# Attention by pairs of heads: fp32 probabilities and values in two halves of TensorE's columns, row sums in four strips

## The chip, the cores and the metric

One core of a Trainium2 chip runs the whole program. The metric is the device time of one execution in microseconds (us). Five engines matter here: TensorE (PE, matmuls; PEld is its loading of weights), VectorE (DVE), ScalarE (ACT), GpSimd (POOL) and SyncE (SP, which starts most DMAs).

## What is computed

The program is a two-block network on 512 tokens of width 1024. The change touches one part of the second block: grouped-query attention of 768 tokens (256 of a context, 512 latent) with 16 query heads of 64 features and 4 key and value heads. Latent queries see all 768 keys, context queries only the 256 of the context.

```python
Q_WIDTH = ATTN_HEADS * HEAD_DIM          # 16 heads of 64
def gqa_attend(q, k, v):
    s = jnp.einsum('bkgqd,bksd->bkgqs', q, k, preferred_element_type=jnp.float32) * (HEAD_DIM ** -0.5)
    p = jax.nn.softmax(s, axis=-1).astype(v.dtype)
    return jnp.einsum('bkgqs,bksd->bkgqd', p, v)
```

All numbers are fp32.

## The kernel before

An ordinary fp32 product is made of three products of a one-pass type, fp32r: a tensor x is split into a high part h (x rounded to fp32r) and a low part l = x - h, and `h·l + l·h + h·h` is summed in PSUM. In the rows such a product stands as three matmuls (L240: `hh,wl`, `hl,wh`, `hh,wh`). A few small matmuls keep plain fp32 operands; each of those leaves two records in the trace, for instance L1489, whose 96 matmuls in the program are 192 records.

`attn_proj` makes Q, K and V, `keys` transposes K into the parts `K2`, and `attend` is the attention. `V` is kept as `Vh` (128 keys x 65: 64 features and a column of ones) and `Vl` (64 features). `attend` is a generator with an order written out by hand at its end:

- `ahead(g)` prepares the pair of heads g = 0 to 7: it transposes the queries, makes their parts `q2` and `q1`, and finds the row maxima `mx` by whole score products (L1738, L1744, with a maximum on DVE each), which go into row 64 of `q1` by DMA so that the score product already has the maximum taken off.
- `scores(h, u)` is one head h and one step u. For u = 0 to 5, step u takes 128 keys against 512 latent queries; step 6 takes the two context key tiles against 256 context queries. Two matmuls (L1765, L1766) fill `st` (two PSUM buffers), ACT takes the exponential into `pr`, and `pr` is split into `ph` and `pl` on ACT, DVE or POOL by a fixed pattern.
- `values(h, u)` adds three matmuls into `acc`: `Vh·pl`, `Vl·ph`, `Vh·ph` (L1787 to L1789). The column of ones makes row 64 of `acc` the softmax's denominator. At u = 5 and u = 6 ACT copies rows 0 to 63 to `O` and row 64 to `sums`.
- `divide(g)` brings the sums to 12 x 128 by DMA, takes the reciprocal, spreads it by matmuls with `pick` (L1815) and multiplies (L1818).

The loop makes scores for (h, u) and values for the step three before; between them it advances `ahead` of the next pair by one yield, and every seventh step it advances `more`, the adaLN products (`mods`): plain fp32 matmuls of 128 x 32 weights (L1489), each in one of four strips of 32 columns of TensorE, `tile_position=(0, c)`, c = 0, 32, 64, 96.

A scheduler decides the final order on each engine from this program, so what stands side by side in the code need not stand side by side on an engine.

Of the kernel before, what the change touches and what calls it, by code (L numbers as in the profile page):

```python
# [9 lines left out]
F32 = mybir.dt.float32  # L10
F32R = mybir.dt.float32r
U32 = mybir.dt.uint32
AF = mybir.ActivationFunctionType
ALU = mybir.AluOpType
# [3 lines left out]
P = 128  # L18
D = 1024
L = 512  # L20
EPS = 1e-6
MIX = 512
C64 = 64
# [1612 lines left out]

def attn_proj(b, st, hs, t0, tabs, p2, w, Q, K, V):


    nc = b.nc  # L1640
    order = [4, 5, 0, 1, 2, 3]

    def take(i, t, acc):
        tab = tabs[t]
        t += t0
        i = order[i]
        a = acc.rearrange("p (h d) -> p h d", d=C64)
        if i == 5:
            h, l = (z[:, t, :, :C64] for z in V)
            nc.scalar.copy(h, a)  # L1650
            nc.vector.tensor_tensor(l, a, h.bitcast(F32), op=ALU.subtract)
            return
        sq = p2.tile([P, 4, C64], F32, tag="sq", name="sq")
        nc.scalar.activation(sq, a, AF.Square)
        s = p2.tile([P, 4], F32, tag="s", name="s")
        nc.vector.tensor_reduce(s, sq, axis=AX.X, op=ALU.add)
        o = (Q[i] if i < 4 else K)[:, t]
        n = 0 if i < 4 else 1
        if tab is None:
            nc.vector.tensor_tensor(o, a, w[:, 2 * n].unsqueeze(1).to_broadcast([P, 4, C64]), op=ALU.mult)  # L1660
        else:
            cos, sin = (z.unsqueeze(1).to_broadcast([P, 4, C64]) for z in tab[2 * n : 2 * n + 2])
            nc.vector.tensor_tensor(o, a, cos, op=ALU.mult)
            r = p2.tile([P, 4, C64], F32, tag="r", name="r")
            half = lambda z, f: z.rearrange("p h (x f i) -> p h x f i", x=2, f=2)[:, :, :, f]
            for f in range(2):
                nc.vector.tensor_tensor(half(r, f), half(a, 1 - f), half(sin, f), op=ALU.mult)
            nc.gpsimd.tensor_tensor(o, o, r, op=ALU.add)
        z = 1.0 / C64 if n else 1.0
        nc.vector.tensor_scalar(s, s, z, z * C64 * EPS, op0=ALU.mult, op1=ALU.add)  # L1670
        b.power(s, 4)
        nc.gpsimd.tensor_tensor(o, o, s.unsqueeze(2).to_broadcast([P, 4, C64]), op=ALU.mult)

    return st.tokens(b.a["w_qkv"], 8, hs, range(len(tabs)), order, take)


# [16 lines left out]
def attend(b, Q, K2, V, out, high, low, p2, psc, ctx, more):  # L1693

    nc = b.nc
    Vh, Vl = V
    T, n0 = 6 * P, 2 * P  # L1700
    old, new = slice(0, n0), slice(n0, T)
    ready = {}
# [51 lines left out]
            nc.sync.dma_start(q1[a][64:65].bitcast(F32).rearrange("o (t q) -> o t q", q=P), mr[6 * a : 6 * a + 6].bitcast(F32))  # L1754
        yield

    def scores(h, u):

        q2, q1 = (q[h % 2] for q in ready[h // 2][:2])
        K1 = ready[h // 2][2]  # L1760
        kv = h // 4
        p = pss.tile([P, 512], F32, tag="st", name="st")
        for k, q, o in [(u, new, p)] if u < 6 else [(k, old, p[:, k * n0 : (k + 1) * n0]) for k in range(2)]:
            c = slice(k * P, (k + 1) * P)
            nc.tensor.matmul(o, K1[:, c], q1[:, q], start=True, stop=False)  # L1765
            nc.tensor.matmul(o, K2[:, kv, c], q2[:, q], start=False, stop=True)  # L1766
        pr = p4.tile([P, 512], F32, tag="pr", name="pr")
        nc.scalar.activation(pr, p, AF.Exp)
        ph, pl = (pp.tile([P, 512], F32R, tag=z, name=z) for z in ("ph", "pl"))
        n = 7 * h + u  # L1770
        if n % 5 == 3:
            nc.scalar.copy(ph, pr)
        else:
            (nc.vector if n % 5 == 1 else nc.gpsimd).tensor_scalar(ph, pr, 1.0, 0.0, op0=ALU.mult, op1=ALU.add)
        (nc.vector if n % 3 == 1 else nc.gpsimd).tensor_tensor(pl, pr, ph.bitcast(F32), op=ALU.subtract)
        return ph, pl

    accs, sums, O, L = {}, {}, {}, {}

    def values(h, u, ph, pl):  # L1780
        kv = h // 4
        if u in (0, 6):
            accs[h] = psa.tile([P, 512], F32, tag="acc", name="acc")[:65, : 4 * P if u == 0 else n0]
        acc = accs[h]
        for k, x in [(u, slice(0, 512))] if u < 6 else [(k, slice(k * n0, (k + 1) * n0)) for k in range(2)]:
            first, last = k == 0, k == (1 if u == 6 else 5)
            nc.tensor.matmul(acc, Vh[:, k, kv], pl[:, x], start=first, stop=False)  # L1787
            nc.tensor.matmul(acc[:64], Vl[:, k, kv], ph[:, x], start=False, stop=False)
            nc.tensor.matmul(acc, Vh[:, k, kv], ph[:, x], start=False, stop=last)  # L1789
        if u < 5:  # L1790
            return
        g, r = h // 2, h % 2 * 64
        if u == 5 and h % 2 == 0:
            sums[g] = p1.tile([65, T], F32, tag="s", name="sums")
            O[g] = po.tile([P, T], F32, tag="O", name="O")
        at = new if u == 5 else old
        nc.scalar.copy(O[g][r : r + 64, at], acc[:64])
        nc.scalar.copy(sums[g][r : r + 1, at], acc[64:])
        if u == 6 and h % 2:
            parts.append(divide(h // 2))  # L1800
            next(parts[-1])

    def divide(g):
        inv = p2.tile([12, P], F32, tag="s", name="s")
        for a in range(2):
            nc.sync.dma_start(inv[6 * a : 6 * a + 6], sums[g][64 * a : 64 * a + 1].rearrange("o (t q) -> o t q", q=P))
        nc.vector.reciprocal(inv, inv)
        if g % 2 == 0:
            L[g // 2] = low.tile([P, 2, T], F32R, tag="l", name="ol")
        out.append((high.tile([P, T], F32R, tag="h", name="oh"), L[g // 2][:, g % 2]))  # L1810
        yield
        for c0, c1 in ((2, 6), (0, 2)):
            r = psc.tile([P, 512], F32, tag="ps", name="rt")[:, : (c1 - c0) * P]
            for t in range(c0, c1):
                nc.tensor.matmul(r[:, (t - c0) * P : (t - c0 + 1) * P], pick[:, t], inv, start=True, stop=True)  # L1815
            s = slice(c0 * P, c1 * P)
            o = O[g][:, s]
            nc.vector.tensor_tensor(o, o, r, op=ALU.mult)  # L1818
            b.parts(*(z[:, s] for z in out[g]), o)
        yield  # L1820
# [1 line left out]
    yield from ahead(0)  # L1822
    yield
    pq = b.pool("atq", 2, ctx=ctx)
    pp = b.pool("atp", 5, ctx=ctx)
    p4 = b.pool("at4", 4, ctx=ctx)
    pss, psa = (b.pool(f"ps2{n}", k, PSUM, ctx=ctx) for n, k in (("s", 2), ("v", 2)))
    po = b.pool("ato", 2, ctx=ctx)
    p1 = b.pool("at1", 1, ctx=ctx)
    pick = p1.tile([12, 6, P], F32, name="pick")  # L1830
    for t in range(6):
        nc.scalar.copy(pick[:, t].rearrange("p (a i) -> p a i", a=2),
                       b.ident[:12, t : t + 7 : 6].unsqueeze(2).to_broadcast([12, 2, 64]))
    todo = [(h, u) for h in range(16) for u in range(7)]
    made, parts, lead, side = [], [], 3, iter(())
    for i in range(len(todo) + lead):
        if i < len(todo):
            h, u = todo[i]
            made.append(scores(h, u))
            if h % 2 == 0 and u == 0 and h < 14:  # L1840
                side = ahead(h // 2 + 1)
        next(side, None)
        if i % 7 == 3:
            next(more, None)
        if i >= lead:
            values(*todo[i - lead], *made[i - lead])
            made[i - lead] = None
            if i == len(todo) + lead - 1 or i % 14 == 12 and i > 14:
                next(parts.pop())
    run(more)  # L1850

# [238 lines left out]
def block2(b, st, X, h, late, old_, c, out, ctx):  # L2090


    nc = b.nc
    n = 256
    T = n + L
    old, new = slice(0, n), slice(n, T)
# [7 lines left out]
    with ExitStack() as c0:  # L2104
# [3 lines left out]
        with ExitStack() as c1:  # L2108
            kp = b.pool("kv", 1, ctx=c1, side="right")
            K2 = kp.tile([P, 4, T], F32R, name="K2")  # L2110
            V = kp.tile([P, 6, 4, C64 + 1], F32R, name="Vh"), kp.tile([P, 6, 4, C64], F32R, name="Vl")
            nc.gpsimd.memset(V[0][:, :, :, C64:].bitcast(F32), 1.0)
            K = kp.tile([P, 6, 4, C64], F32, name="K")
            at2 = b.pool("at2", 2, ctx=c1, side="right")
            ps = b.pool("ps2a", 4, PSUM, ctx=c1)
            with ExitStack() as c2:
# [4 lines left out]
                p2 = b.pool("ap2", 2, ctx=c2, side="right")  # L2121
# [6 lines left out]
                o = []  # L2128
# [18 lines left out]
            with ExitStack() as c2:  # L2147
                st.banks("acc2b", 4, c2)
                parts, h = cut(*mods), space()
# [5 lines left out]
        ps = b.pool("ps2c", 2, PSUM, ctx=cp)  # L2155
# [21 lines left out]
    with ExitStack() as c1:  # L2177
        with ExitStack() as c:
            st.banks("acc2e", 3, c)
            ps = b.pool("ps2e", 5, PSUM, ctx=c)  # L2180
# [14 lines left out]
            o = hgrn(b, st, *h, ps, c, lb, lambda: late(wl, ps), result, add)  # L2195
        st.banks("acc2g", 6, ctx)
        ps = b.pool("ps2g", 2, PSUM, ctx=ctx)
        wk = b.pool("wk3", 2, ctx=ctx)
        parts, h = [Part(X, s, s, m) for s in HALVES], space()
        norms = [lambda p=p: p.norm(b, h, m.g2, m.sh2, wk, ps) for p in parts]  # L2200
        last = st.weights(b.a["hg_wo"][:, :, 7].rearrange("m p c -> p m c"), 8)
# [48 lines left out]
```

## Time and profile before

| | |
|---|---|
| median of 3 runs | 3248.89 us (3246.69 to 3251.31) |
| the profiled execution's own time | 3249.31 us |
| its span in the profile | 3247.5 us |
| mean granted TensorE clock | 0.98 |
| busy: PE, PEld, DVE, ACT, POOL | 96%, 81%, 56%, 37%, 24% of the span |
| busy in 1496 to 1723 us (the attention loop): PE, DVE, ACT, POOL | 218.86, 161.72, 134.62, 171.21 of 227 us |

The profile's rows give an engine, a source line, an operation, the output tile and its inputs, and the shape. In a group of instructions the numbers behind the bar are busy time, mean duration of one, and idle time before them with its releaser. Matmul records overlap: the end of one is modelled and reaches past the start of the next, so what a matmul costs TensorE is read from one start to the next.

### The profile page before, as it was taken

The page shows a single profiled execution, that of the slowest core. Times are in us where ns is not written, and L with a number is a line of the kernel's source. Part 1 is how long each engine was busy: PE and PEld are TensorE (multiplying, and loading weights), DVE is VectorE, ACT ScalarE, POOL GpSimd, SP SyncE. Part 2 cuts the span into 40 slices and gives each one's busy share as a digit, 9 for nine tenths or more (in the row PEclk, how much of TensorE's full clock was granted, in tenths as well). Part 3 has the DMA queues.
Part 4 walks back from the last instruction along what each step waited for, and adds up shares of the span by engine and source line. Part 5 has one row for each costly group of instructions (what it writes and reads, how often), then busy time and mean ns, then how long its engine had stood idle before and what let it go on. Part 6 is the DMA issues. An engine that isn't in the chain of part 4 may idle for free.

```text
span 3247.5 us, 51132 instructions
## 1 busy us (share of the span) xinstructions
PE 3114.1 (96%) x20456; PEld 2645.7 (81%) x20456; DVE 1827.2 (56%) x3179; ACT 1190.2 (37%) x2121; POOL 778.1 (24%) x827
## 2 busy tenths in 40 slices
PE   7999989989999999899999999999999999889998
PEld 6777777778887787897668988888889998788887
DVE  6554476455556464677775685323555555753434
ACT  4333333324344242545664321211344444332223
POOL 3222032131040000468875100000323222310003
PEclk9999998999999999999999999999999999989999
DMA  2111333233345332432223474222331111123333
GB/s 99 56 57 46 97 88 95 75 105 119 111 125 178 94 97 91 122 118 79 79 92 117 140 233 156 62 65 61 99 103 50 53 53 46 58 73 97 94 97 115
DMA packets 130910, 308.17 MB, mean 95 GB/s; under 512 B 34016, under 2 KB 55216, under 8 KB 130160
## 3 DMA queue, kind: packets, MB, share of 16 engines
q1 hardware_dynamic: 126032, 293.95, 29.2%
q10 hardware_dynamic: 4640, 10.95, 0.9%
q8 instruction: 161, 2.64, 0.3%
q14 instruction: 77, 0.63, 0.1%
HBM read 295.18 MB, written 8.39 MB: 93 GB/s over the span
## 4 chain that ended last, share of the span: by engine, by line
PE 83%; DVE 8%; issue 2%; DMA 2%; ACT 2%; POOL 2%; SPq 0%; DVEq 0%; POOLq 0%; ACTq 0%
PE acc L240 57%; DVE wl L204 3%; PE ps L524 3%; PE gate L1194 3%; PE acc L262 2%; PE acc L263 2%; PE acc L264 2%; PE ps L1979 2%; PE mods L1489 1%; PE ss L346 1%; ACT wh L200 1%; PE sc L1744 1%; PE st L1765 1%; DMA w<-in_ada_dram 1%; PE st L1766 1%
## 5 line engine op out<-in xcount | busy, mean ns | idle before, releaser
L240 PE MATMUL acc<-hh,wl 128*128 128x512 f32 (+1 forms) x2296 | 761.7, 364 | 7.8 <-DVE wl L204 5.6
L240 PE MATMUL acc<-hh,wh 128*128 128x512 f32 (+1 forms) x2296 | 757.9, 361 | 0.0
L240 PE MATMUL acc<-hl,wh 128*128 128x512 f32 (+1 forms) x2296 | 757.2, 361 | 0.0
L200 ACT CAST wh<-raw 128x1024 fp32r<-128x1024 f32 (+4 forms) x584 | 480.4, 826 | 650.4 <-PE acc L240 412.4
L204 DVE TENSOR_TENSOR wl<-raw,wh 128x1024 fp32r<-128x1024 f32 (+3 forms) x584 | 555.6, 954 | 254.5 <-ACT wh L200 248.0
L204 POOL TENSOR_TENSOR wl<-raw,wh 128x512 fp32r<-128x512 f32 (+1 forms) x120 | 169.9, 1419 | 1295.6 <-ACT wh L200 583.3
L240 PEld LDWEIGHTS acc<-hh,wl 128*128 128x128 f32 x2296 | 402.5, 189 | 85.5 <-DVE wl L204 9.4
L240 PEld LDWEIGHTS acc<-hh,wh 128*128 128x128 f32 x2296 | 402.4, 189 | 68.3 <-issue 0.9
L240 PEld LDWEIGHTS acc<-hl,wh 128*128 128x128 f32 x2296 | 402.1, 189 | 65.5 <-issue 0.8
L240 PE MATMUL acc<-mh,wl 128*128 128x512 f32 (+1 forms) x848 | 265.9, 339 | 15.4 <-DVE wl L204 14.9
L240 PE MATMUL acc<-mh,wh 128*128 128x512 f32 (+1 forms) x848 | 260.6, 332 | 0.0
L240 PE MATMUL acc<-ml,wh 128*128 128x512 f32 (+1 forms) x848 | 260.2, 332 | 0.2 <-DVE ml L340 0.2
L240 PEld LDWEIGHTS acc<-mh,wl 128*128 128x128 f32 x848 | 150.9, 188 | 37.8 <-DVE wl L204 19.9
L240 PEld LDWEIGHTS acc<-ml,wh 128*128 128x128 f32 x848 | 151.4, 189 | 17.6 <-DVE ml L340 0.4
L240 PEld LDWEIGHTS acc<-mh,wh 128*128 128x128 f32 x848 | 150.9, 188 | 17.4
L1603 ACT ACTIVATE t<-acc 128x512 f32<-128x512 f32 x66 | 34.7, 527 | 343.9 <-PE acc L240 339.8
L1555 DVE SCALAR_TENSOR_TENSOR X<-acc,mod,X 128x256 f32<-128x256 f32 (+1 forms) x112 | 65.4, 593 | 159.1 <-PE acc L240 159.1
L1604 DVE SCALAR_TENSOR_TENSOR t<-t,acc 128x512 f32<-128x512 f32 x66 | 39.4, 597 | 162.2 <-ACT t L1603 162.1
L262 PE MATMUL acc<-wl,hh 128*128 128x256 f32 x448 | 126.6, 284 | 1.7 <-DVE wl L204 1.0
L263 PE MATMUL acc<-wh,hl 128*128 128x256 f32 x448 | 126.9, 284 | 0.0
L264 PE MATMUL acc<-wh,hh 128*128 128x256 f32 x448 | 126.7, 285 | 0.0
L1605 DVE TENSOR_TENSOR t<-t,acc 128x512 f32<-128x512 f32 x66 | 39.4, 598 | 137.4 <-PE acc L240 136.9
(604 smaller groups left out, 5839.5 us busy)
## 6 DMA issues: line engine op xcount, KB each, us to landing
raw<-in_ffn_in_dram SPq DMA_DIRECT2D x88, 512.0 KB, 3.5
ada<-in_ada_dram SPq DMA_DIRECT2D x48, 512.0 KB, 3.9
w<-in_ada_dram SPq DMA_DIRECT2D x48, 512.0 KB, 4.3
raw<-in_ffn_w_up_dram SPq DMA_DIRECT2D x44, 512.0 KB, 3.5
raw<-in_ffn_out_dram SPq DMA_DIRECT2D x32, 512.0 KB, 3.5
raw<-in_hg_w_dram SPq DMA_DIRECT2D x32, 512.0 KB, 3.6
raw<-in_ffn_out_dram SPq DMA_DIRECT2D x40, 384.0 KB, 3.1
raw<-in_w_qkv_dram SPq DMA_DIRECT2D x24, 512.0 KB, 3.5
```

Of the source, the lines that this page charges most:

```text
L200: nc.scalar.copy(h, raw)
L204: e.tensor_tensor(l[:, s], raw[:, s], h[:, s].bitcast(F32), op=ALU.subtract)
L240: nc.tensor.matmul(z[0], w[:, k], z[x], start=k == 0 and n == 0, stop=k == ks - 1 and n == 2)
L262: nc.tensor.matmul(acc, xh, wl, start=k == 0, stop=False)
L263: nc.tensor.matmul(acc, xl, wh, start=False, stop=False)
L264: nc.tensor.matmul(acc, xh, wh, start=False, stop=k == ks - 1)
L524: nc.tensor.matmul(out(r, ci), lhsT(r, ci), rhs(r, ci), start=start, stop=stop)
L1194: nc.tensor.matmul(acc, w[:, 0], x, start=k + i == 0, stop=k == 7 and i == 2)
L1555: return lambda i, acc: b.nc.vector.scalar_tensor_tensor(X[:, i], acc, gate[:, i : i + 1], X[:, i], op0=ALU.mult, op1=ALU.add)
L1604: nc.vector.scalar_tensor_tensor(t, t, 1.0, a, op0=ALU.add, op1=ALU.mult)
L1605: nc.vector.tensor_tensor(t, t, u, op=ALU.mult)
L1979: nc.tensor.matmul(p[:, c], kc[:, c * P : (c + 1) * P], qc[:, c * P : (c + 1) * P], start=True, stop=True)
```

## The change

Heads are treated in pairs. `pr` stays in fp32 and is no longer split; `V` stays in fp32 as one tile without a column of ones. For each key tile the values of both heads of a pair are two plain fp32 matmuls of 64 columns, the first head's in TensorE's columns 0 to 63 and the second head's in 64 to 127, into the two halves of one `acc`. The denominators are made apart: DVE adds the probabilities of three key tiles at a time (`three`), and `add_up` multiplies two such sums of each head by a 128 x 32 matrix of ones, in four strips of 32 columns; for the context queries it takes the four pieces of `pr` as they are. `divide` adds the two sums of a head. The loop runs over 8 pairs x 7 steps with the values two steps behind the scores, and advances `ahead` twice a step and `more` every third step.

```diff
@@ attn_proj
         if i == 5:
-            h, l = (z[:, t, :, :C64] for z in V)
-            nc.scalar.copy(h, a)
-            nc.vector.tensor_tensor(l, a, h.bitcast(F32), op=ALU.subtract)
+            nc.scalar.copy(V[:, t], a)
             return
@@ attend
-    def scores(h, u):
...
-        pr = p4.tile([P, 512], F32, tag="pr", name="pr")
-        nc.scalar.activation(pr, p, AF.Exp)
-        ph, pl = (pp.tile([P, 512], F32R, tag=z, name=z) for z in ("ph", "pl"))
-        n = 7 * h + u
-        if n % 5 == 3:
-            nc.scalar.copy(ph, pr)
-        else:
-            (nc.vector if n % 5 == 1 else nc.gpsimd).tensor_scalar(ph, pr, 1.0, 0.0, op0=ALU.mult, op1=ALU.add)
-        (nc.vector if n % 3 == 1 else nc.gpsimd).tensor_tensor(pl, pr, ph.bitcast(F32), op=ALU.subtract)
-        return ph, pl
+    def scores(g, u):
+
+        q2s, q1s, K1 = ready[g]
+        kv = g // 2
+        out = []
+        for q2, q1 in zip(q2s, q1s):
+            p = pss.tile([P, 512], F32, tag="st", name="st")
...
+            out.append(pp.tile([P, 512], F32, tag="pr", name="pr"))
+            nc.scalar.activation(out[-1], p, AF.Exp)
+        return out
+
+    def add_up(g, at, prs):
+
+        acc = psc.tile([P, 512], F32, tag="ps", name="den")[:, : at.stop - at.start]
+        for n, pr in enumerate(prs):
+            c = 32 * n
+            nc.tensor.matmul(acc[c : c + 32], ones, pr, start=True, stop=True, tile_position=(0, c))
+        nc.scalar.copy(sums[g][:, at], acc)
@@ values
         for k, x in [(u, slice(0, 512))] if u < 6 else [(k, slice(k * n0, (k + 1) * n0)) for k in range(2)]:
-            first, last = k == 0, k == (1 if u == 6 else 5)
-            nc.tensor.matmul(acc, Vh[:, k, kv], pl[:, x], start=first, stop=False)
-            nc.tensor.matmul(acc[:64], Vl[:, k, kv], ph[:, x], start=False, stop=False)
-            nc.tensor.matmul(acc, Vh[:, k, kv], ph[:, x], start=False, stop=last)
+            for a, pr in enumerate(prs):
+                nc.tensor.matmul(acc[a * 64 : a * 64 + 64], V[:, k, kv], pr[:, x], start=k == 0,
+                                 stop=k == (1 if u == 6 else 5), tile_position=(0, 64 * a))
+        if u < 6:
+            if u % 3 == 0:
+                three[u // 3] = prs
+            else:
+                made = []
+                for z, pr in zip(three[u // 3], prs):
+                    o = ps_.tile([P, 512], F32, tag="sm", name="sm") if u % 3 == 1 else z
+                    nc.vector.tensor_tensor(o, z, pr, op=ALU.add)
+                    made.append(o)
+                three[u // 3] = made
...
-        nc.scalar.copy(O[g][r : r + 64, at], acc[:64])
-        nc.scalar.copy(sums[g][r : r + 1, at], acc[64:])
+        nc.scalar.copy(O[g][:, at], acc)
+        if u == 5:
+            waiting.append(lambda z=[z for two in zip(three[0], three[1]) for z in two]: add_up(g, new, z))
+        else:
+            add_up(g, old, [pr[:, k * n0 : (k + 1) * n0] for pr in prs for k in range(2)])
@@ divide
+        two = p2.tile([12, 2, P], F32, tag="s2", name="s2")
+        for a in range(2):
+            for n in range(2):
+                r = 64 * a + 32 * n
+                nc.sync.dma_start(two[6 * a : 6 * a + 6, n], sums[g][r : r + 1].rearrange("o (t q) -> o t q", q=P))
+        nc.vector.tensor_tensor(inv, two[:, 0], two[:, 1], op=ALU.add)
@@ the loop
-    pp = b.pool("atp", 5, ctx=ctx)
-    p4 = b.pool("at4", 4, ctx=ctx)
+    pp = b.pool("atp", 8, ctx=ctx)
+    ps_ = b.pool("ats", 6, ctx=ctx)
...
-    made, parts, lead, side = [], [], 3, iter(())
+    made, parts, waiting, lead, side = [], [], [], 2, iter(())
...
-        next(side, None)
-        if i % 7 == 3:
+        for _ in range(2):
+            next(side, None)
+        if i % 3 == 1:
             next(more, None)
+        if waiting:
+            waiting.pop()()
```

The order that the scheduler makes of it differs from the code's. First TensorE in the kernel before, in the loop's middle; the numbers behind the names tell buffers apart, and the size at the end is the output's rows by columns. The values of one step of one head are the three rows L1787 to L1789.

```order
L1744 MATMUL sc_16203<-K2_12780,q2_16081 128x384
L1765 MATMUL st_16191<-q1_15758,K1_15431 128x512
L1766 MATMUL st_16191<-q2_15756,K2_12780 128x512
L1744 MATMUL sc_16218<-K2_12780,q2_16081 128x384
L1787 MATMUL acc_16187<-pl_16078,Vh_12781 65x512
L1788 MATMUL acc_16187<-ph_16077,Vl_12782 64x512
L1789 MATMUL acc_16187<-ph_16077,Vh_12781 65x512
L1765 MATMUL st_16209<-q1_15758,K1_15431 128x512
L1766 MATMUL st_16209<-q2_15756,K2_12780 128x512
```

TensorE in the changed kernel, in the middle of a pair's steps. L1788 are now the values; `acc_16128` is one pair's accumulator, and its matmuls belong in turn to the first and the second head (`pr_16109` and `pr_16114` are the two heads of one step, `pr_16134` is the first head's next).

```order
L1788 MATMUL acc_16128<-pr_16048,V_12781 64x512
L1743 MATMUL sc_16122<-K2_12780,q2_16009 128x384
L1765 MATMUL st_16131<-q1_15750,K1_15752 128x512
L1766 MATMUL st_16131<-q2_15748,K2_12780 128x512
L1788 MATMUL acc_16128<-pr_16109,V_12781 64x512
L1743 MATMUL sc_16125<-K2_12780,q2_16009 128x384
L1495 MATMUL mods_16062<-ct_all_58,mods_16180 128x2 x4
L1743 MATMUL sc_16141<-K2_12780,q2_16009 128x384
L1765 MATMUL st_16136<-q1_15751,K1_15752 128x512
L1766 MATMUL st_16136<-q2_15749,K2_12780 128x512
L1788 MATMUL acc_16128<-pr_16114,V_12781 64x512
```

The two heads' matmuls of a step, neighbours in the code, have three to six matmuls of all 128 columns between them. The end of the same pair on TensorE is the second place: `acc_16289` is the context queries' accumulator (step 6), `den` the denominators (L1778), first of the latent and then of the context queries.

```order
L1788 MATMUL acc_16289<-pr_16241,V_12781 64x256
L1788 MATMUL acc_16289<-pr_16234,V_12781 64x256
L1788 MATMUL acc_16289<-pr_16241,V_12781 64x256
L1830 MATMUL rt_16215<-s_16102,pick_14462 128x128 x4
L1830 MATMUL rt_16223<-s_16102,pick_14462 128x128 x2
L1749 MATMUL mt_16244<-ct_all_58,mx_16050 12x128
L1778 MATMUL den_16283<-sm_16154,ones_14460 32x512
L1778 MATMUL den_16283<-sm_16252,ones_14460 32x512
L1778 MATMUL den_16283<-sm_16156,ones_14460 32x512
L1778 MATMUL den_16283<-sm_16254,ones_14460 32x512
L1778 MATMUL den_16295<-pr_16234,ones_14460 32x256 x2
L1778 MATMUL den_16295<-pr_16241,ones_14460 32x256 x2
```

Here the strips stand next to each other.

## Rows read from the trace of the kernel before

**Rows 1.** The page: the chain that ended last, by engine.

```profile
PE 83%; DVE 8%; issue 2%; DMA 2%; ACT 2%; POOL 2%; SPq 0%; DVEq 0%; POOLq 0%; ACTq 0%
```

**Rows 2.** Stretches of the loop: us; busy PE, PEld, DVE, ACT, POOL; clock; DMA.

```profile
1496.00:1723.00 227.00, 218.86 (x1153) 151.12 (x1153) 161.72 (x278) 134.62 (x262) 171.21 (x178) 0.98 0.25 80
1500.00:1690.00 190.00, 186.50 (x999) 127.66 (x999) 142.50 (x255) 117.83 (x232) 145.47 (x154) 1.00 0.27 85
1690.00:1715.00 25.00, 20.73 (x98) 13.64 (x99) 14.91 (x15) 14.21 (x26) 21.91 (x19) 0.93 0.24 77
1715.00:1733.00 18.00, 15.64 (x90) 14.78 (x90) 6.47 (x10) 4.62 (x8) 3.47 (x2) 0.72 0.18 58
```

**Rows 3.** Groups of instructions with their shapes, 1496 to 1723 us: TensorE.

```profile
L1787 PE MATMUL acc<-pl,Vh 128*65 128x512 f32 x96 | 39.6, 412 | 2.4 <-POOL pl L1775 1.8 <-DVE pl L1775 0.5
...
L1789 PE MATMUL acc<-ph,Vh 128*65 128x256 f32 x32 | 9.0, 280 | 0.0
L1489 PE MATMUL mods<-ada,silu 128*32 128x512 f32 x128 | 25.0, 603 | 0.3 <-DVE mx L1739 0.3
```

**Rows 4.** Timeline of TensorE from 1552 us: start, length, instruction.

```profile
1552.41 0.28 PE L1787 MATMUL acc<-pl,Vh 128*65 128x256 f32 x1
1552.53 0.28 PE L1788 MATMUL acc<-ph,Vl 128*64 128x256 f32 x1
...
1553.00 0.40 PE L1766 MATMUL st<-q,K 128*128 128x512 f32 x1
1553.33 1.91 PE L1489 MATMUL mods<-ada,silu 128*32 128x512 f32 x12
1555.17 0.44 PE L1787 MATMUL acc<-pl,Vh 128*65 128x512 f32 x1
1555.45 0.39 PE L1788 MATMUL acc<-ph,Vl 128*64 128x512 f32 x1
1555.67 0.40 PE L1789 MATMUL acc<-ph,Vh 128*65 128x512 f32 x1
1555.91 0.34 PE L1744 MATMUL sc<-K,q 128*128 128x384 f32 x1
```

**Rows 5.** Timeline of TensorE around two shorter visits to the strips.

```profile
1501.24 0.39 PE L1766 MATMUL st<-q,K 128*128 128x512 f32 x1
1501.56 1.06 PE L1489 MATMUL mods<-ada,silu 128*32 128x512 f32 x6
1502.55 0.50 PE L1765 MATMUL st<-q,K 65*128 65x512 f32 x1
1502.89 0.40 PE L1766 MATMUL st<-q,K 128*128 128x512 f32 x1
...
1585.23 1.05 PE L1489 MATMUL mods<-ada,silu 128*32 128x512 f32 x4
1586.21 0.44 PE L1744 MATMUL sc<-K,q 128*128 128x384 f32 x1
```

**Rows 6.** Who waited for whom on TensorE, 1496 to 1723 us: total, times, longest.

```profile
PE acc L1787 <- POOL pl L1775: 4.0, 7, 0.9
PE acc L1787 <- DVE pl L1775: 0.5, 1, 0.5
```

**Rows 7.** Groups of the other engines in the same stretch.

```profile
L1775 POOL TENSOR_TENSOR pl<-pr,ph 128x512 fp32r<-128x512 f32 x75 | 101.5, 1361 | 11.9 <-ACT ph L1772 6.8 <-DVE ph L1774 2.7
...
L1774 POOL TENSOR_SCALAR ph<-pr 128x512 fp32r<-128x512 f32 x67 | 47.2, 710 | 29.5 <-ACT pr L1768 27.6 <-issue 1.3
L1775 DVE TENSOR_TENSOR pl<-pr,ph 128x512 fp32r<-128x512 f32 x37 | 37.4, 1010 | 8.9 <-POOL ph L1774 7.2 <-ACT ph L1772 1.4
L1774 DVE TENSOR_SCALAR ph<-pr 128x512 fp32r<-128x512 f32 x23 | 18.1, 785 | 13.2 <-ACT pr L1768 13.2
...
L1818 DVE TENSOR_TENSOR O<-O,rt 128x512 f32<-128x512 f32 x8 | 5.5, 683 | 10.1 <-PE rt L1815 10.1
```

**Rows 8.** The chain that ended last, in order of time, behind the loop's end.

```profile
1714.25 6.43 PE acc L240 x39
```

More of the change, by code (lines that the diff above doesn't have):

```diff
@@ L1698, in attend @@
     nc = b.nc
-    Vh, Vl = V
     T, n0 = 6 * P, 2 * P
@@ L1755, in ahead @@
         yield
-    def scores(h, u):
[L1759 to L1766, printed above, removed]
-        pr = p4.tile([P, 512], F32, tag="pr", name="pr")
-        nc.scalar.activation(pr, p, AF.Exp)
-        ph, pl = (pp.tile([P, 512], F32R, tag=z, name=z) for z in ("ph", "pl"))
-        n = 7 * h + u
-        if n % 5 == 3:
-            nc.scalar.copy(ph, pr)
-        else:
-            (nc.vector if n % 5 == 1 else nc.gpsimd).tensor_scalar(ph, pr, 1.0, 0.0, op0=ALU.mult, op1=ALU.add)
-        (nc.vector if n % 3 == 1 else nc.gpsimd).tensor_tensor(pl, pr, ph.bitcast(F32), op=ALU.subtract)
-        return ph, pl
@@ L1778, in attend @@
-    accs, sums, O, L = {}, {}, {}, {}
-    def values(h, u, ph, pl):
-        kv = h // 4
+    def scores(g, u):
[4 more added lines that the diff above has]
+            p = pss.tile([P, 512], F32, tag="st", name="st")
+            for k, q, o in [(u, new, p)] if u < 6 else [(k, old, p[:, k * n0 : (k + 1) * n0]) for k in range(2)]:
+                c = slice(k * P, (k + 1) * P)
+                nc.tensor.matmul(o, K1[:, c], q1[:, q], start=True, stop=False)
+                nc.tensor.matmul(o, K2[:, kv, c], q2[:, q], start=False, stop=True)
+            out.append(pp.tile([P, 512], F32, tag="pr", name="pr"))
+            nc.scalar.activation(out[-1], p, AF.Exp)
+        return out
@@ L1782, in values @@
+    accs, sums, O, L, three = {}, {}, {}, {}, {}
+    def add_up(g, at, prs):
[4 more added lines that the diff above has]
+        nc.scalar.copy(sums[g][:, at], acc)
+    def values(g, u, prs):
+        kv = g // 2
         if u in (0, 6):
-            accs[h] = psa.tile([P, 512], F32, tag="acc", name="acc")[:65, : 4 * P if u == 0 else n0]
@@ L1784, in values @@
-        acc = accs[h]
+            accs[g] = psa.tile([P, 512], F32, tag="acc", name="acc")[:, : 4 * P if u == 0 else n0]
+        acc = accs[g]
         for k, x in [(u, slice(0, 512))] if u < 6 else [(k, slice(k * n0, (k + 1) * n0)) for k in range(2)]:
-            first, last = k == 0, k == (1 if u == 6 else 5)
-            nc.tensor.matmul(acc, Vh[:, k, kv], pl[:, x], start=first, stop=False)
-            nc.tensor.matmul(acc[:64], Vl[:, k, kv], ph[:, x], start=False, stop=False)
-            nc.tensor.matmul(acc, Vh[:, k, kv], ph[:, x], start=False, stop=last)
+            for a, pr in enumerate(prs):
+                nc.tensor.matmul(acc[a * 64 : a * 64 + 64], V[:, k, kv], pr[:, x], start=k == 0,
+                                 stop=k == (1 if u == 6 else 5), tile_position=(0, 64 * a))
@@ L1790, in values @@
+        if u < 6:
[8 more added lines that the diff above has]
+                three[u // 3] = made
         if u < 5:
             return
-        g, r = h // 2, h % 2 * 64
-        if u == 5 and h % 2 == 0:
-            sums[g] = p1.tile([65, T], F32, tag="s", name="sums")
+        at = new if u == 5 else old
@@ L1795, in values @@
+        if u == 5:
+            sums[g] = p1.tile([P, T], F32, tag="s", name="sums")
             O[g] = po.tile([P, T], F32, tag="O", name="O")
-        at = new if u == 5 else old
-        nc.scalar.copy(O[g][r : r + 64, at], acc[:64])
-        nc.scalar.copy(sums[g][r : r + 1, at], acc[64:])
-        if u == 6 and h % 2:
-            parts.append(divide(h // 2))
+        nc.scalar.copy(O[g][:, at], acc)
+        if u == 5:
+            waiting.append(lambda z=[z for two in zip(three[0], three[1]) for z in two]: add_up(g, new, z))
+        else:
+            add_up(g, old, [pr[:, k * n0 : (k + 1) * n0] for pr in prs for k in range(2)])
+            parts.append(divide(g))
@@ L1801, in values @@
             next(parts[-1])
     def divide(g):
+        two = p2.tile([12, 2, P], F32, tag="s2", name="s2")
[3 more added lines that the diff above has]
+                nc.sync.dma_start(two[6 * a : 6 * a + 6, n], sums[g][r : r + 1].rearrange("o (t q) -> o t q", q=P))
         inv = p2.tile([12, P], F32, tag="s", name="s")
-        for a in range(2):
-            nc.sync.dma_start(inv[6 * a : 6 * a + 6], sums[g][64 * a : 64 * a + 1].rearrange("o (t q) -> o t q", q=P))
+        nc.vector.tensor_tensor(inv, two[:, 0], two[:, 1], op=ALU.add)
@@ L1829, in attend @@
     p1 = b.pool("at1", 1, ctx=ctx)
+    ones = p1.tile([P, 32], F32, name="ones")
+    nc.gpsimd.memset(ones, 1.0)
     pick = p1.tile([12, 6, P], F32, name="pick")
@@ L1833, in attend @@
                        b.ident[:12, t : t + 7 : 6].unsqueeze(2).to_broadcast([12, 2, 64]))
-    todo = [(h, u) for h in range(16) for u in range(7)]
-    made, parts, lead, side = [], [], 3, iter(())
+    todo = [(g, u) for g in range(8) for u in range(7)]
+    made, parts, waiting, lead, side = [], [], [], 2, iter(())
     for i in range(len(todo) + lead):
         if i < len(todo):
[L1838 to L1841, printed above, removed]
-        next(side, None)
-        if i % 7 == 3:
+            g, u = todo[i]
+            made.append(scores(g, u))
+            if u == 0 and g < 7:
+                side = ahead(g + 1)
+        for _ in range(2):
+            next(side, None)
+        if i % 3 == 1:
             next(more, None)
+        if waiting:
+            waiting.pop()()
         if i >= lead:
-            values(*todo[i - lead], *made[i - lead])
+            values(*todo[i - lead], made[i - lead])
             made[i - lead] = None
-            if i == len(todo) + lead - 1 or i % 14 == 12 and i > 14:
+            if i == len(todo) + lead - 1 or i % 7 == 5 and i > 8:
                 next(parts.pop())
@@ L2110, in block2 @@
             K2 = kp.tile([P, 4, T], F32R, name="K2")
-            V = kp.tile([P, 6, 4, C64 + 1], F32R, name="Vh"), kp.tile([P, 6, 4, C64], F32R, name="Vl")
-            nc.gpsimd.memset(V[0][:, :, :, C64:].bitcast(F32), 1.0)
+            V = kp.tile([P, 6, 4, C64], F32, name="V")
             K = kp.tile([P, 6, 4, C64], F32, name="K")
```

## The prediction, made before the changed kernel was run

> **What bounds the kernel now.** I read the chain of waits first: TensorE holds 83% of it [rows 1]. The change lies in the attention loop, so I went on to that loop's busy times: TensorE is busy 218.86 of 227 us there, POOL 171, DVE 162, ACT 135 [rows 2]. No other engine is near full, and TensorE's waits for the splitting of the probabilities, the work that the change deletes, come to 4.0 + 0.5 us in the whole loop [rows 6]. So the elementwise side has at most some 5 us to give; what the change is worth is decided by the time that its matmuls take on TensorE, and by nothing else. That time is read from start to start in the timeline.
>
> **The price of a value step before.** Three fp32r matmuls of 512 columns follow each other at 0.22 to 0.24 us [rows 4], 0.70 us for one head and one key tile; those of 256 columns come every 0.12 us. There are 96 triples of 512 columns and 32 of 256 (the three lines have the same counts) [rows 3]: 96 x 3 x 0.233 + 32 x 3 x 0.1175 = 67.0 + 11.3 = 78.3 us.
>
> **The price of plain fp32 in strips.** The adaLN products in the same loop are that form. Twelve records, that is six matmuls in four strips, hold TensorE from 1553.33 to 1555.17, 1.84 us [rows 4]; four records (two matmuls) 0.98 us, six records (three matmuls) 0.99 us [rows 5]. So strips that stand side by side run together: two or three cost the same, and six in four strips need two rounds. A round more costs 1.84 - 0.99 = 0.85 us, two passes of 0.43 us: an fp32 matmul of 512 columns takes 0.86 us however few columns of the array it uses, and its twin is free only if it is next to it.
>
> **Entering and leaving.** Around the one-round visit, the start before it is 1501.24 and the start of the second matmul after it 1502.89 [rows 5]: 1.65 us, of which 2 x 0.23 belong to the two fp32r matmuls. The visit costs 1.19 us: 0.86 of passes and 0.33 around them (0.09 before the first strip, 0.13 behind the last, 0.11 more before the next matmul reaches its usual pitch). Around the two-round visit it is 1555.45 - 1553.00 - 0.46 - 1.72 = 0.27 us [rows 4]. I take 0.32; the loop's weights after a visit are mostly 128 columns wide, as in the first case. The Trainium skill, "TensorEngine Tiling (Array Packing)", section "Key Properties", says that a change of tiling mode drains TensorE. The trace agrees for fp32 strips, by those 0.27 to 0.33 us. It doesn't for every narrow matmul: L1788 before has 64 columns too, but in fp32r, and starts 0.22 to 0.23 us after its neighbour like any other [rows 4]. If the rule held for all narrow matmuls, each of the 128 L1788 before would already pay such a visit and the change would add fewer; if the new matmuls behaved like L1788, none would be paid (a rival, below).
>
> **The sum on TensorE.** In the order of the changed program the twins don't stand together: of the 96 value matmuls of 512 columns not one has its twin next to it; score and maximum products of all 128 columns lie between, which leave no columns free for a strip. Counted over the loop:
> - values of 512 columns: 96 x 0.86 = 82.4 us (82.4 at 0.858);
> - values of 256 columns: 32 matmuls, of which some share a pass, 20 rounds of 0.43 us = 8.6 us;
> - denominators: 8 rounds of 0.86 and a few broken ones, 8.2 us for the latent queries, 9 half rounds or 3.9 us for the context ones;
> - 21 changes between 64 and 32 columns inside a visit. No row shows one; they lie between 0 and a whole 0.32 us, I take the 0.1 us that entering costs: 2 us (0 to 6.7);
> - visits: 119 in place of 18 (those of the adaLN products alone), 101 x 0.32 = 32 us (27 to 33 by the two rows).
>
> That is 82.4 + 8.6 + 8.2 + 3.9 + 2 + 32 = 137 us where 78.3 stood: 59 us more. Scores, maxima, transposes and adaLN products are the same in number.
>
> **What comes off.** The splits disappear: 148.7 us on POOL, 55.5 on DVE, some casts on ACT. DVE gets 64 additions of 128 x 512, at the 0.68 us of L1818 44 us [rows 7], so its load falls slightly while the loop grows. ACT's copies of `acc` halve in number (one of 128 rows for two of 64 and two of 1). `ahead`'s maxima and the exponentials stay. All of that lies beside TensorE, which then has over 280 us of work; what can be given back is its 4.5 us of waits for the splits [rows 6], and the lost clock at the loop's end, where these waits sit: 0.93 over 25 us and 0.72 over 18 us [rows 2], 1.7 + 5.0 us, if TensorE no longer pauses there. I take 4.5 + 4 = 8.5 of these 11. The rest of the edits cost nothing visible: the two DMAs more per pair in `divide` run while TensorE is in the next pair's steps; behind the last pair the products of attn_wo cover that chain for 6.43 us [rows 8], and if that were too short, it would be about 2 us once. `attn_proj` loses six DVE subtractions beside its matmuls.
>
> So +59 - 8.5 = +50.5 us on the profiled 3249.31 us, which lies within 0.5 us of the runs' median: 3300 us.
>
> **The rivals.**
> - The halves run side by side, as the code is written. Then a step of a pair is one visit of 1.18 us in place of two, against 1.40 before. Taking 48 visits of 1.18 off the 59: +2 us on TensorE, and with 8.5 to 11 given back 3240 to 3243 us, faster by 0.2 to 0.3%. It is no slower than before from about 43 of the 48 pairs that start within some ns of each other. For it speaks that the strips of L1489 do overlap [rows 4, 5]; against it, that the order puts full-width matmuls between the twins and that the order of before is what the trace of before shows, row by row. The Trainium skill's page on tiling, "Theoretical Speedup", gives up to twice the rate for operands of at most 64 columns; that is this rival. 5%.
> - Entering and leaving is free for 64 columns, as it is for the fp32r L1788. Then 59 falls to 27, 3268 us. Against it: the plain fp32 strips pay it whichever strip is first. 10%.
> - TensorE waits for the denominators: `den` needs DVE's additions of the pair's last step, which queue behind the maxima on DVE, and the `den` tile shares four PSUM buffers with the maxima. At 1 to 2 us for each of 8 pairs, 8 to 16 us more: 3308 to 3316 us. 12%.
> - The clock falls where TensorE works on half its columns. At the lower of the two levels every pass in the loop takes twice as long, some 280 us more, near 3570 us. The clock stayed at 1.00 from 1500 to 1690 us with 18 visits in it [rows 2]; lone halves are not shown. 4%.
> - The forecast itself, 3283 to 3308 us: 69%.
>
> **How the numbers follow.** A measurement of this kernel can tell about 0.2% (6.5 us) from no change. Only the first rival and mishaps of the sum come near or under 3255 us: faster 0.04, same 0.03, slower 0.93. The range takes in the second rival's edge and the third: 3270 to 3320 us.
>
> **What would show it.** In the profile after: L1788 as 256 records, of which those of 512 columns start in twos 0.43 us apart, both of the same head; 1.15 to 1.2 us from the matmul before such a pair to the steady pitch behind it; TensorE busy through the loop, now about 275 us long; hardly a wait of TensorE for POOL or for `pr`. POOL almost empty there. If two heads' records start within 0.01 us of each other, the forecast is wrong on the fast side; if L1788's passes come 0.86 us apart, or `den` waits for `sm`, on the slow side.

## The result, and the profile after

| | before | changed |
|---|---|---|
| median of 4 runs | 3250.1 us | 3308.4 us (3307.2 to 3310.88) |
| ratio to before | | 1.0182, 95% interval 1.0164 to 1.0199 |
| span of the profiled execution | 3247.5 us | 3306.4 us |
| first score matmul to last `rt` matmul | 1496.12 to 1721.94, 225.8 us | 1498.46 to 1783.21, 284.8 us |

The change makes the kernel slower by 58 us (forecast: 50.5), and all of it lies in the attention loop, which grew by 58.9 us; the rest of the program takes the same time within a fraction of a us. The chain of waits of the changed kernel, by engine, against [rows 1]:

```profile
PE 84%; DVE 7%; DMA 3%; issue 2%; ACT 2%; POOL 1%; SPq 0%; ACTq 0%; POOLq 0%; DVEq 0%
```

TensorE is still what everything waits for. Busy times of the changed kernel by stretch, in the columns of [rows 2]:

```profile
1498.00:1784.00 286.00, 281.23 (x1153) 122.22 (x1153) 152.64 (x291) 109.07 (x208) 21.14 (x37) 0.97 0.20 64
1500.00:1637.00 137.00, 135.80 (x556) 57.65 (x554) 75.97 (x145) 52.63 (x103) 10.64 (x21) 0.98 0.23 74
1637.00:1649.00 12.00, 11.23 (x43) 5.66 (x42) 5.91 (x13) 5.20 (x12) 1.99 (x4) 0.57 0.17 46
1649.00:1784.00 135.00, 132.66 (x556) 57.78 (x555) 69.23 (x130) 50.41 (x94) 6.59 (x10) 1.00 0.17 56
```

POOL fell from 171 to 21 us, DVE and ACT lost some too, and none of it shortened the loop: TensorE is busy for 281 of 286 us. The clock stood at its lower level in two stretches, for the loop's first 6 us and for 10 us behind 1637 (0.57 on average from 1637 to 1649). The values' and denominators' groups, against [rows 3], and the new additions on DVE:

```profile
L1788 PE MATMUL acc<-pr,V 128*64 128x512 f32 x192 | 103.8, 622 | 0.0
L1797 DVE TENSOR_TENSOR sm<-pr 128x512 f32<-128x512 f32 x32 | 22.0, 689 | 20.6 <-ACT pr L1768 20.5
L1797 DVE TENSOR_TENSOR sm<-sm,pr 128x512 f32<-128x512 f32 x32 | 21.9, 685 | 11.9 <-ACT pr L1768 11.8
L1788 PE MATMUL acc<-pr,V 128*64 128x256 f32 x64 | 13.1, 397 | 0.0
L1778 PE MATMUL den<-sm,ones 128*32 128x512 f32 x64 | 11.5, 662 | 0.0
L1778 PE MATMUL den<-pr,ones 128*32 128x256 f32 x64 | 6.1, 420 | 0.0
```

The 64 additions took DVE 44 us, as forecast. A piece of TensorE's timeline in the changed kernel shows where the time went; it is to be read against [rows 4, 5]:

```profile
1621.21 0.40 PE L1766 MATMUL st<-q,K 128*128 128x512 f32 x1
1621.54 1.07 PE L1788 MATMUL acc<-pr,V 128*64 128x512 f32 x2
1622.54 0.45 PE L1743 MATMUL sc<-K,q 128*128 128x384 f32 x1
1622.82 0.39 PE L1765 MATMUL st<-q,K 65*128 65x512 f32 x1
1623.05 0.40 PE L1766 MATMUL st<-q,K 128*128 128x512 f32 x1
1623.38 1.07 PE L1788 MATMUL acc<-pr,V 128*64 128x512 f32 x2
1624.38 0.44 PE L1743 MATMUL sc<-K,q 128*128 128x384 f32 x1
```

Each L1788 row is one matmul of one head (two records, its two passes), alone between full-width matmuls. From 1621.21 to 1622.82 are 1.61 us; less the usual 0.23 of L1766 and 0.18 of L1743, one half costs 1.20 us, where three fp32r matmuls cost 0.70. The next half starts 1.84 us later and pays the same again; the halves belong in turn to the two heads. TensorE's waits in the loop, against [rows 6]:

```profile
PE st L1765 <- DMA q<-mr: 2.8, 3, 1.7
PE mods L1489 <- DMA ada<-in_ada_dram: 1.2, 1, 1.2
PE rt L1830 <- DVE s L1822: 0.5, 1, 0.5
PE sc L1743 <- POOL q L1730: 0.4, 1, 0.4
PE mt L1749 <- DVE mx L1747: 0.4, 1, 0.4
```

The waits for the splits are gone, and nothing large took their place.

### The profile page after: what moved, and what is told of

It is laid out like the page before. It is cut to its first block, busy times and chain, and to the rows that moved or that the text cites. A ratio compares the mean times of both kernels' runs of the same rounds, so it can differ in the third digit from the quotient of the medians.

```text
span 3306.4 us, 50922 instructions
## 1 busy us (share of the span) xinstructions
PE 3172.1 (96%) x20456; PEld 2613.7 (79%) x20456; DVE 1816.6 (55%) x3185; ACT 1164.4 (35%) x2067; POOL 625.5 (19%) x685
## 4 chain that ended last, share of the span: by engine, by line
PE 84%; DVE 7%; DMA 3%; issue 2%; ACT 2%; POOL 1%; SPq 0%; ACTq 0%; POOLq 0%; DVEq 0%
PE acc L240 56%; PE acc L1788 3%; PE ps L524 3%; PE gate L1194 3%; DVE wl L204 2%; PE acc L262 2%; PE acc L264 2%; PE acc L263 2%; PE ps L1999 2%; PE st L1765 1%; PE sc L1743 1%; PE mods L1489 1%; PE st L1766 1%; ACT wh L200 1%; PE ss L346 1%
## 5 line engine op out<-in xcount | busy, mean ns | idle before, releaser
L1788 PE MATMUL acc<-pr,V 128*64 128x512 f32 (+1 forms) x256 | 115.0, 566 | 0.0
```

Of the source, the lines that this page charges most:

```text
L1788: nc.tensor.matmul(acc[a * 64 : a * 64 + 64], V[:, k, kv], pr[:, x], start=k == 0, stop=k == (1 if u == 6 else 5), tile_position=(0, 64 * a))
```

## The experiments

The theory after the result: a value half costs TensorE a whole fp32 matmul and a whole visit to the strips (the time around a stretch of narrow matmuls that lies between full-width ones), because the scheduler put full-width matmuls between the twins. Rivals: fp32 halves are slow even side by side; entering and leaving is cheap and the passes are all; the denominators' waits; or waits elsewhere.

**Twins together by a fixed order, and its control.** Every TensorE instruction of the loop is queued behind the one that the code has before it (an order of issue, no wait), in the changed kernel and, as a control, in the kernel before.

```diff
...
+    def in_order():
+        nonlocal last, mark
+        for x in traced[mark:]:
+            if x.engine == mybir.EngineType.PE:
+                if last is not None:
+                    b.tc.add_manual_dep(x, last.name, mybir.DependencyInfo(
+                        mybir.DependencyClass.NoSync, mybir.DependencyReason.DATA), reason="in order")
+                last = x
+        mark = len(traced)
+
     for i in range(len(todo) + lead):
+        in_order()
...
```

Expected of the changed kernel so ordered: 

> The changed kernel with TensorE held to the code's order in the attention loop, nothing else: counted in the order of the program, every value matmul now stands beside its twin, and the visits to the column strips fall from 119 to 55. Theory (a half that stands alone pays a whole fp32 matmul and a whole visit): TensorE's work in the loop falls by some 72 us; a fixed order gives up to 25 us of that back as waits. 3236 to 3261 us. Rival (halves of 64 columns don't run together even side by side, only entering and leaving is saved): 64 visits x 0.32 = 20 us, 3288 us.

Expected of the control: 

> Control: the kernel before with the same fixed order on TensorE in the loop. Its adaLN products then make 8 visits in place of 18: 10 us less work on TensorE, less what the fixed order costs in waits (0 to 15 us): 3240 to 3255 us. If it is much faster than that, the order and not the halves would explain a fast e1; if much slower, the fixed order itself is dear.

Measured: 3305.7 us (ratio 1.0166, 1.0149 to 1.0182) and, for the control, 3300.69 us (1.0151, 1.0137 to 1.0164). Both expectations were wrong, and the control says why: the fixed order itself costs 50 us. TensorE's longest waits in the control between 1480 and 1810 us:

```profile
PE mods L1489 <- DMA ada<-in_ada_dram: 25.2, 8, 3.9
PE sc L1744 <- POOL q L1731: 5.9, 5, 1.6
PE mt L1750 <- DVE mx L1748: 3.5, 5, 1.7
```

An adaLN product that waits for its weights now holds up everything behind it, and around the end of each of these eight pauses the clock fell: 58 us of this loop at the lower level, against 10 in the kernel before. With the order the same, the halves cost 5 us more than the three products (3305.7 against 3300.7), not 58; but two slow kernels prove little, so the order was narrowed.

**Twins together, the rest free, with its control.** Only `scores` and `values` are held to the code's order; all else may still move. Here `in_order` runs the function that it is given and queues only the TensorE instructions that this makes.

```diff
...
-            made.append(scores(g, u))
+            in_order(lambda: made.append(scores(g, u)))
...
-            values(*todo[i - lead], made[i - lead])
+            in_order(lambda: values(*todo[i - lead], made[i - lead]))
...
```

> The changed kernel with only its scores and values held to the code's order on TensorE; maxima, transposes, adaLN products and denominators stay free, so that no adaLN product waits for its DMA at the head of the queue. 48 of the 48 twins stand side by side, 74 visits in place of 119. Theory (a lone half is what the time went to): the work on TensorE falls by 57 us, waits rise by 0 to 10 us: 3252 to 3262 us. Rival (the time is the strips' own, together or apart): 3285 us or more.

Measured: 3262.76 us (ratio 1.0036, 1.0022 to 1.0051), 46 us less than the changed kernel and 0.8 above the range of the expectation. TensorE's timeline in this run:

```profile
1619.83 0.39 PE L1766 MATMUL st<-q,K 128*128 128x512 f32 x1
1620.15 1.08 PE L1788 MATMUL acc<-pr,V 128*64 128x512 f32 x4
1621.16 0.80 PE L1743 MATMUL sc<-K,q 128*128 128x384 f32 x3
1621.79 0.40 PE L1765 MATMUL st<-q,K 65*128 65x512 f32 x1
```

Four records, both heads, take 1.01 us from the first start to the next matmul, where two records of one head took 1.00 in the changed kernel. Side by side the second half takes no time of its own; over the 40 visits of one pair alone the median is 1.21 us. That refutes the first rival. The control, the kernel before with the same order for its scores and values:

> Control for the twins-only run: the kernel before with its scores and values held to the code's order on TensorE. If that order costs nothing by itself, 3246 to 3254 us; if it is what keeps the twins-only run 12 us over the kernel before, 3258 to 3264 us.

Measured: 3249.01 us (0.9999, 0.999 to 1.0009): this order is free, so the 46 us are the twins' doing. What keeps the twins-only run 12 us above the kernel before is, by its size, the clock; no run puts that to the test. The same stretch of the loop, first in the kernel before, then in the twins-only run:

```profile
1496.00:1722.00 226.00, 218.10 (x1150) 150.68 (x1150) 160.83 (x277) 134.21 (x261) 171.21 (x178) 0.98 0.25 80
```

```profile
1494.00:1734.00 240.00, 234.02 (x1153) 117.93 (x1153) 146.68 (x289) 107.98 (x207) 21.27 (x37) 0.92 0.24 76
```

0.92 in place of 0.98 is 36.7 us at the lower level in place of 10.2. At half the clock, half of the difference is lost, 13 us (an estimate), of the 14 us by which the loop of this run is longer (239.8 against 225.8 us).

**The visits by themselves.** The values as full-width fp32 matmuls: nothing side by side, but no visits for them (V twice in 128 columns, an accumulator for each head, each head's half of the rows is copied out; for the context queries these accumulators share the buffers of the maxima).

```diff
...
-                nc.tensor.matmul(acc[a * 64 : a * 64 + 64], V[:, k, kv], pr[:, x], start=k == 0,
-                                 stop=k == (1 if u == 6 else 5), tile_position=(0, 64 * a))
+                nc.tensor.matmul(acc[a], V[:, k, kv], pr[:, x], start=k == 0, stop=k == (1 if u == 6 else 5))
...
```

> The changed kernel with its values as full-width fp32 matmuls: V stands twice in 128 columns, each head has an accumulator of its own and takes its half of the rows. The fp32 passes of the values stay, the visits fall from 119 to 33. Theory (a visit costs 0.32 to 0.34 us beside its passes): 28 us less than the changed kernel, 3278 to 3286 us. Rival (entering and leaving is cheap, the passes are all): 3303 to 3309 us.

Measured: 3285.7 us (1.0109, 1.0095 to 1.0123), 22.7 us less than the changed kernel, near the forecast. The expectation took the passes to stay the same. Those of the 512 columns do; those of 256 no longer share any, 32 rounds of 0.43 us in place of the prediction's 20, 5 us more (an estimate), which is what lies between the 28 us of the expectation and the 23 measured. A full-width fp32 matmul shows no entering in this run:

```profile
1566.78 0.40 PE L1767 MATMUL st<-q,K 128*128 128x512 f32 x1
1567.01 1.02 PE L1790 MATMUL acc<-pr,V 128*128 128x512 f32 x2
```

It starts 0.23 us after its neighbour like any fp32r matmul, so the visit belongs to the strips and not to fp32. Entering and leaving costs about what was read from the adaLN products, and the column halves as scheduled were dearer than no halves at all.

**Plain fp32 without strips or denominators.** The kernel before, with one fp32 product over 65 columns for the three.

```diff
...
-            nc.tensor.matmul(acc, Vh[:, k, kv], pl[:, x], start=first, stop=False)
-            nc.tensor.matmul(acc[:64], Vl[:, k, kv], ph[:, x], start=False, stop=False)
-            nc.tensor.matmul(acc, Vh[:, k, kv], ph[:, x], start=False, stop=last)
+            nc.tensor.matmul(acc, V[:, k, kv], pr[:, x], start=first, stop=last)
...
```

> The kernel before, with one plain fp32 matmul over 65 columns of V (64 features and the ones) in place of the three fp32r ones, no strips, no splitting and no separate denominators. Passes alone: 96 x (0.858 - 0.70) + 32 x (0.43 - 0.353) = 18 us more on TensorE, and 0 to 3 us of waits for the splits come back (8.5 by the prediction's term): 3264 to 3268 us, or 3259 by the prediction's term.

Measured: 3270.62 us (1.0057, 1.0037 to 1.0077). That is 20 us over the kernel before, 2.6 above the expected range; the interval takes in 12 to 25 us. It agrees with the 18 us that were worked out for the passes alone, 0.86 for 0.70 us, and leaves room for little or nothing that comes back for the splits that fell away.

**The splits by themselves.**

```diff
...
-        pr = p4.tile([P, 512], F32, tag="pr", name="pr")
-        nc.scalar.activation(pr, p, AF.Exp)
-        ph, pl = (pp.tile([P, 512], F32R, tag=z, name=z) for z in ("ph", "pl"))
...
-        return ph, pl
+        ph = pp.tile([P, 512], F32R, tag="ph", name="ph")
+        nc.scalar.activation(ph, p, AF.Exp)
+        return ph, ph
...
```

> The kernel before without the splitting: the exponential is written as fp32r at once and stands for both parts of the probabilities (the low part is left out), so TensorE's work is unchanged and only the work of POOL, DVE and ACT falls. Theory: 8.5 us of waits and lost clock come back, 3238 to 3246 us. Rival (all of it was hidden): 3247 to 3252 us.

Measured: 3250.26 us (0.9999, 0.999 to 1.0008). My theory was wrong here, and the rival held: nothing came back. TensorE's waits between 1480 and 1810 us in this run:

```profile
PE st L1765 <- ACT ph L1768: 6.3, 6, 1.8
PE st L1765 <- DMA q<-mr: 2.2, 2, 1.7
```

The 4.5 us of waits for the splits [rows 6] turned into 6.3 us of waits for the exponential; here the clock was 0.99 in the loop, and the loop as long as before.

**The denominators by themselves.**

```diff
...
-        acc = psc.tile([P, 512], F32, tag="ps", name="den")[:, : at.stop - at.start]
-        for n, pr in enumerate(prs):
-            c = 32 * n
-            nc.tensor.matmul(acc[c : c + 32], ones, pr, start=True, stop=True, tile_position=(0, c))
-        nc.scalar.copy(sums[g][:, at], acc)
+        nc.scalar.activation(sums[g][:, at], prs[0][:, : at.stop - at.start], AF.Exp, scale=0.0)
...
```

> The changed kernel without the denominators' matmuls (ACT writes ones in their place, the output is not normalised). By the order they are 16 us of TensorE's time with their changes of width and visits, and TensorE's waits for DVE in them are 3 us: 3288 to 3293 us. If the waits for the sums were what made the change slow, it would fall much further, to 3270 us or less.

Measured: 3293.32 us (1.0133, 1.012 to 1.0146), 15.1 us less than the changed kernel, 0.3 above the expected range. They cost their matmuls' time; they aren't what made the change slow.

**Towards a faster version.** Three runs build on the twins. First, values ahead of the other work in each step, and the denominators in the fixed order too: 

> The same, with the values written ahead of the maxima and adaLN products in each step, and the denominators in the fixed order too: 68 visits. By the work on TensorE 62 us less than the changed kernel, waits 0 to 10 us more: 3246 to 3256 us, the kernel before within its uncertainty. Rival as for the run before: 3280 us or more.

Then the values of two steps in one visit:

```diff
...
+            held.append(i - lead)
+            if todo[i - lead][1] in (1, 3, 5, 6):
+                in_order(lambda: [values(*todo[j], made[j]) for j in held])
...
```

> The same, with the values of two steps made in one visit, where the visits' own price is halved once more: 46 visits in place of 68, with the same passes. Theory (a visit costs 0.34 us beside its passes): 7 us less than the run before it, 3239 to 3249 us. Rival (what is left are waits, not visits): as the run before it, 3246 to 3256 us.

Measured: 3261.89 us (1.003, 1.0018 to 1.0042) and 3262.41 us (1.0033, 1.0022 to 1.0045): no gain over the twins alone, and both expectations missed. The visits did fall, and a visit of two pairs takes 2.06 us (median of 22) for 2 x 1.21; but what was saved came back as waits and lost clock (43.8 us of the loop at the lower level). TensorE's waits in the loop with the values in twos:

```profile
PE st L1765 <- DMA q<-mr: 7.9, 5, 2.3
PE mt L1749 <- DVE mx L1747: 5.1, 6, 1.7
```

They lie where one pair ends and the next one's maxima aren't there yet, so these were prepared sooner, three yields of `ahead` a step on top of the run before it, with a control in the kernel before (three yields in two steps in place of two):

```diff
...
-        for _ in range(2):
+        for _ in range(3):
             next(side, None)
...
```

> The values in twos, with the preparation of the next pair (maxima and transposes) advanced three times a step in place of twice, so that it is done two steps before the pair needs it. In the run before, TensorE waits 7.9 us for the maxima's DMA and 5.1 us for DVE at the pairs' ends, and the granted clock falls to 0.5 there at each pair, 37 us in all in the loop. Theory (the lack of cover at the pairs' ends costs what the halves gained): 10 to 25 us less than the 3262.4 us before, 3237 to 3252 us. Rival (the clock falls for the strips' sake): 3257 to 3266 us.

> Control for the run before: the kernel before with its preparation advanced three times in two steps in place of twice. Its waits of that kind are 0.6 us for DVE and 1.7 us for the DMA of the first pair: same as before, 3246 to 3253 us.

Measured: 3260.19 us (1.0033, 1.0021 to 1.0045), where the rival said 3257 to 3266, and the control 3254.34 us (1.001, 1.0001 to 1.0018), 1.3 above its range. The first row of waits with the maxima sooner, and a place where one of them falls:

```profile
PE mt L1749 <- DVE mx L1747: 10.2, 7, 2.2
```

```profile
1572.51 1.44 PE L1743 MATMUL sc<-K,q 128*128 128x384 f32 x5
1575.57 0.38 PE L1749 MATMUL mt<-ct_all,mx 128*12 128x128 f32 x1 [1.61 <-DVE mx L1747]
```

The wait for the DMA fell from 7.9 to 1.7 us and a wait for DVE, now given its maxima in a bunch (five products in a row), took its place; the clock in the loop stayed near 0.92. So the time was not bought back, and none of the versions beats the kernel before. Halves of fp32r matmuls, three passes of 0.233 us for the 0.86 of one fp32 matmul by [rows 4], were not tried.

## Why the prediction was right, and what of it was off

- **TensorE's work decides, not the elementwise engines.** Right. POOL lost 150 us of work and the loop grew; removing the splits alone changed nothing.
- **The twins don't meet.** Right, and it is the largest part: putting them side by side, and nothing else, took off 46 of the 58 us. The order of the built program was enough to see it, and the trace bears it out: no visit holds two halves of 512 columns, and as a rule two to six full-width matmuls lie between them.
- **A half costs 0.86 + 0.32 us.** 1.18 forecast; the 76 halves of 512 columns that have a visit to themselves show a median of 1.20. The full-width run took off 23 us: 86 fewer visits at 0.32 give 28, less some 5 for the 256-column passes that it no longer shares.
- **A change of width inside a visit** was put at 0.1 us without a row: a half with the four latent denominators behind it takes 2.20 us, 2 x 0.86 of it passes and 0.34 the visit, so it is 0.15.
- **The sum on TensorE** was the mis-sized term: 137 us forecast; by the same reading of starts the trace shows 173.1 us in 119 visits against 27.6 in 18, so 145.5. Of the 8.5 us too many, some 5 are waits and low clock in four visits (1.0 to 1.8 us each over their passes and one entering and leaving), 2 the halves' 0.02 each, 1 the changes of width.
- **What comes off** was put at 8.5 us. The loop outside the visits did shrink by 8.3 us (58.9 = 145.5 - 78.3 - 8.3), but with the 5 us of waits inside visits set against it only 3 remain, and the clock gave nothing back: 16.4 us of the loop at the lower level against 10.2. The run without splits shows that this term couldn't be counted on: a wait of TensorE that goes makes room for the next one, here the exponential's.
- **The rivals.** Free overlap needs the order to allow it, and shows as soon as it does. Free entering is refuted by the starts (1.20 us for a lone half) and by the full-width run. The fp32r L1788 of the kernel before, which paid nothing, is also a matmul without a `tile_position`; no run tells whether its type or that spared it. The rival with 8 to 16 us of waits for the denominators did not come: `den` stands nowhere among TensorE's waits. The 3 us of the expectation above are gaps of 0.3 to 0.8 us between weight loads, while TensorE's matmuls ran on; the run without the denominators took off 15.1, where their matmuls alone were put at 16. A lower clock for lone halves did not happen in the changed kernel (0.97 in its loop).

The Trainium skill, "TensorEngine Tiling (Array Packing)", "Key Properties", says that tiles operate independently and that a change of mode drains the engine. The runs agree with both for fp32 strips (1.21 us for two halves, 1.20 for one, 0.3 us around a visit, none around a full-width fp32 matmul); what TensorE does in these 0.3 us no run shows, and the first helps only matmuls that are next to each other.

## What to carry to other kernels

A narrow fp32 matmul in a strip of columns paid its full passes here (0.86 us for 512 columns) and a visit (0.34 us); what halves this price is a neighbour in another strip, and whether it has one is decided by the order that the scheduler leaves, not by the code. Read that order before counting on overlap, and if the neighbours must stay together, fix their order alone: fixing everything cost 50 us here, fixing scores and values nothing. Work taken from engines that TensorE hardly waits for was worth nothing, and even a wait in the profile need not come back when its cause goes.

## What the runs showed of the hardware that was not expected

Once the twins stood together, TensorE had some 57 us less to do (an estimate: 48 halves of 1.20 us that now run beside their twins), and the granted clock in the loop went to 0.92: 36.7 us at the lower of the two levels (1.2 and 2.4 GHz) against 10.2 in the kernel before and 16.4 in the changed one. With the values in twos the falls came near the end of each pair, every 31 us or so. In that run the engine did this before one of them, at 1609.1 us:

```profile
1604.49 0.44 PE L1743 MATMUL sc<-K,q 128*128 128x384 f32 x1 [0.30 <-DVE m L1745]
1604.96 1.15 PE L1830 MATMUL rt<-s,pick 12*128 12x128 f32 x8
1606.39 1.05 PE L1489 MATMUL mods<-ada,silu 128*32 128x512 f32 x4 [0.28 <-DMA ada<-in_ada_dram]
1607.38 0.71 PE L1830 MATMUL rt<-s,pick 12*128 12x128 f32 x4
1608.01 0.28 PE L1749 MATMUL mt<-ct_all,mx 128*12 128x128 f32 x1
1608.13 1.05 PE L1495 MATMUL mods<-ct_all,mods 128*128 128x2 f32 x8
1609.04 1.48 PE L1720 MATMUL qt<-ct_all,Q 128*128 128x128 f32 x6
```

Small matmuls of few rows or columns stand close together there, with short waits. Whether these, the strips or the waits bring the clock down was not settled. Waits can go with a fall without any halves: in the control of the fixed order each of the eight pauses for adaLN weights, 2.3 to 3.9 us, has a fall around its end. In the twins-only run the one wait of 1.1 us, for adaLN weights, ends where the clock falls at 1575.1, but in the 20 us before the fall at 1605.9 there is none. Preparing the maxima sooner moved the waits and left the clock where it was. That is also why it stays open whether paired halves could beat the kernel before.
